# First up group by K tile, norms through a matrix of 1/2048, and later state outputs in a hybrid streaming step

## The chip, the core and the metric

The kernel runs on one core of one Trainium2 chip. The metric is the device time of one execution in microseconds. TensorE multiplies matrices into PSUM, VectorE (DVE), ScalarE (ACT) and GpSimd (POOL) work element by element, and the queues of SyncE (SP), GpSimd and ScalarE start transfers. Each engine takes its instructions in order and waits for the others through semaphores.

## What is computed

One layer of a streaming encoder for 256 prompt positions and 32 sample positions, held side by side as 288 columns (`NT`), with features on the partitions:

```python
xn = rmsnorm(x, norm_mix_pre)
proj = xn @ w_in                 # [pool 1024 | z 2048 | xBC 2560 | dt 32]
y_pool = pool_mixer(u, ...)      # trailing means, then four 256 x 256 products
y_ssd, new_conv, new_h = ssd_mixer(z, xbc, dt_raw, ...)   # grouped gated RMSNorm at its end
mix = concatenate([y_pool, y_ssd]) @ w_out
x = x + rmsnorm(mix, norm_mix_post)
hn = rmsnorm(x, norm_ffn_pre)
up = hn @ w_up                   # 2048 -> 2 * 5632
up, new_fconv = causal_dwconv(up, hist_fconv, ...)
f = (silu(gate) * val) @ w_down
x = x + rmsnorm(f, norm_ffn_post)
```

The outputs are `x` for both groups and the new caches, among them `new_h`, the SSD states of prompt and sample (128 x 2048 values each here).

## The kernel before

Products are made in fp32 precision from three passes: weights and activations are split into a rounded part (`hi`) and a remainder (`lo`), and `mm3` (L133) adds hi x hi, hi x lo and lo x hi. `fetch_w` (L110) loads a piece of weights into a `raw` tile on SP's queue, `split_w` (L116) makes `whi` on ScalarE and `wlo` on VectorE, 1024 columns at a time, each from a ring of four buffers. `project` (L138) runs a group of output tiles of 128 features over the K tiles in pieces `ksplit`, each tile into a bank of PSUM: five banks `acc` and three banks `aux`, which also hold the sums of norms and other small products.

The stages in order: the first six tiles of the input product, the SSD mixer beside the rest of that product, the pooling branch, the output product of the mixer (`wov`, eight groups of two tiles, L755), the residual and the norm before the FFN (L772 to L800), the FFN in two halves (`up_half`, L853, then the down product, L867 and L943), and the final norm.

Norms need the sum of squares over features, that is over partitions and tiles, for each of the 288 columns. `token_sums` (L472) multiplies the squares (as weights) with one column of `ones`, so that positions land on partitions; `token_rstd` (L483) takes root and reciprocal of three columns; `spread` (L490) turns the result back into 288 columns on all partitions; `copy_out` (L506) takes it out of PSUM where it is needed there. Two grouped norms of the SSD mixer (`rg`, L585 and L595), the norm behind the mixer (`p_m`, `rm`, L772) and the norm ahead of the FFN (`r2`, L800) go this way. The norm at the input (L233) multiplies the full matrix `ones` with the sums.

The states are 2048 columns in four parts j of 512. `state_in` (L709) fetches and scales the inputs through GpSimd's queue, `state_p` (L727) and `state_s` (L737) make the prompt's and the sample's part on TensorE and write them out on SP's queue. They run behind the mixer's output groups 2, 3 and 4; the last part is fetched behind group 6 and made between the sums and the spread of `rm`, with the order pinned (`keep_in_program_order`).

From there `s` runs over 16 feature tiles: x1 = mg * rm + x (two VectorE operations), `hn` in `hi` (ScalarE) and `lo` (VectorE), the square on ScalarE and its addition to `xsum` on VectorE. The first up group (L856) is six tiles in four pieces of four K tiles; it takes `hn` as it comes. Its results are multiplied by `r2` in `fconv` (L811), which is why the product may start ahead of the sums; then come the convolution, the gate (`finish_pair`, L829) and the split of `fa`. `blocks_out` (L167) transposes a finished x1 tile on VectorE into one buffer `blocks` and writes it to DRAM with four transfers, 16 times in the first half. Where several instructions can go, a scheduler sets each engine's order by priority: `ahead` brings weight splits forward, `EVAC` the operations that empty PSUM.

Of the kernel before, what the change touches and what calls it, by code (L numbers as in the profile page):

```python
# [16 lines left out]
P = 128  # L17
# [3 lines left out]
NS = 32  # L21
# [22 lines left out]
def body(  # L44
# [12 lines left out]
    w_out,  # L57
    w_up,
# [51 lines left out]
    def fetch_w(view, kb, nk, c0, nc_):  # L110
        raw = wpool.tile([P, nk, nc_], F32, tag="raw", name="raw")
        with tc.high_priority(offset=ahead[0]):
            sp.dma_start(out=raw, in_=view[:, c0 // 256, kb : kb + nk, :])
        return raw
# [52 lines left out]
    def blocks_out(d, t, src, pool_):  # L167
# [12 lines left out]
    ones = const.tile([P, P], F32, name="ones")  # L180
    pool.memset(ones, 1.0)
    tri = const.tile([P, P], F32, name="tri")
    pool.affine_select(
        out=tri, in_=ones, pattern=[[1, P]], compare_op=ALU.is_ge, fill=0.0, base=0, channel_multiplier=-1
# [47 lines left out]

    def input_rstd():  # L233
        p_ = aux([P, NT], "prs")
        pe.matmul(p_, ones, xsum, start=True, stop=True)
        act.activation(rstd, p_, AF.Sqrt, bias=eps_t, scale=1.0 / D_MODEL)
        dve.reciprocal(rstd, rstd)
# [187 lines left out]
    elast = const.tile([P, HEADS + 24], F32, name="elast")  # L425
# [46 lines left out]
    def token_sums(p_, sq, first_, last_, pin=False):  # L472


        for b, o in enumerate((0, P, NT - P)):
            ins = pe.matmul(
                p_[:, b : b + 1], sq[:, o : o + P], ones[:, 0:1],
                start=first_ and b == 0, stop=last_ and b == 2, skip_group_check=True,
            )
            if pin:  # L480
                tc.keep_in_program_order(ins)

    def token_rstd(p_, scale, name):  # L483

        o = const.tile([P, 3], F32, tag="trs", bufs=2, name=name)
        act.activation(o, p_[:, 0:3], AF.Sqrt, bias=eps_t, scale=scale)
        dve.reciprocal(o, o)
        return o

    def spread(rs, name, pin=False):  # L490

        p_ = aux([P, NT], name)
        for b, (o, n) in enumerate(BLK):
            ins = pe.matmul(
                p_[:, o : o + n], rs[:, b : b + 1].broadcast_to([P, P]), ident[:, P - n :], start=True, stop=True
            )
            if pin:
                tc.keep_in_program_order(ins)
        return p_

    def rstd_all(sq, scale, name):
        p_ = aux([P, 4], "psum_t")
        token_sums(p_, sq, True, True)
        return spread(token_rstd(p_, scale, name), name)

    def copy_out(p_, pool_, name):  # L506
        o = pool_.tile([P, NT], F32, tag="spread", bufs=3, name=name)
        act.activation(o, p_, AF.Copy)
        return o
# [63 lines left out]
    for i in range(NX // 2):  # L573
# [21 lines left out]
    rg.append(copy_out(rstd_all(gsum[1], 0.25 / 1024, "rg1"), const, "rg1_"))  # L595
# [141 lines left out]
    def state_s(j, x, h, pin=False):  # L737
# [7 lines left out]
    late_in = []  # L745

    def mix_before(g):
        def hook(kb, n):
            if g == 0 and kb == 0:
                pool_group(0)  # L750
            if g == 7 and kb == 0:
                token_sums(p_m, msum, True, False)
        return hook

    for grp in ((0, 1), (2,), (3,), (4,), (5,), (6,), (7,)):  # L755
# [4 lines left out]
        if 2 <= grp[0] < 5:  # L760
# [3 lines left out]
        elif grp[0] == 6:  # L764
            late_in = state_in(3)
# [11 lines left out]
    late = []  # L777
    for s in range(KD + 1):
        if s < KD:
            tc.keep_in_program_order(dve.tensor_tensor(x1[s], x1[s], rm, op=ALU.mult))  # L780
            tc.keep_in_program_order(dve.tensor_tensor(x1[s], x1[s], xT[:, s, :], op=ALU.add))
        if s:
            t = s - 1
            a = atile("hn")
            hi = act.activation(a[:, 0, :], x1[t], AF.Copy, scale=g_ffn_pre[:, t : t + 1])
            lo = dve.scalar_tensor_tensor(  # L786
                a[:, 1, :], x1[t], g_ffn_pre[:, t : t + 1], a[:, 0, :].bitcast(F32),
                op0=ALU.mult, op1=ALU.subtract,
            )
            tc.keep_in_program_order(lo)  # L790
            if t == 0:
                late.extend((hi, lo))
            if t == 0:
                act.activation(xsum, x1[t], AF.Square)
            else:
                q = op_.tile([P, NT], F32, tag="sq", bufs=2, name="sq")
                act.activation(q, x1[t], AF.Square)
# [254 lines left out]
```

## Time and profile before

| | us |
|---|---|
| median of 3 runs (1341.77 to 1343.39) | 1343.27 |
| the profiled execution | 1341.92 |
| its span, first to last instruction | 1340.2 |
| VectorE busy | 875.3 |
| ScalarE busy | 662.4 |
| GpSimd busy | 217.6 |

The profile comes from one execution on the hardware. A line of the chain of waits gives start, length, engine, what is written and the source line; a line of a timeline gives start, length, engine, line, operation, out<-in with partitions x elements, count, and in brackets how long the engine sat idle before and what ended it; a group of instructions gives busy time, mean ns of one and idle time. PE is TensorE, PEld its weight loads. An fp32 matmul without the split stands as two records.

### The profile page before, as it was taken

How to read it: one execution, taken by the hardware profiler on the slowest of the kernel's cores; microseconds unless marked ns; L12 is line 12 of the kernel's file. 1: busy time of each engine (PE TensorE's matmuls, PEld its weight loads, DVE VectorE, ACT ScalarE, POOL GpSimd, SP SyncE). 2: the span in 40 equal slices, each digit the busy share in tenths (PEclk: the TensorE clock that was granted, in tenths of full speed). 3: DMA queues.
4: the chain of work that ended last, by engine and by line, in shares of the span. 5: the costliest groups of instructions: out<-in, count | busy, mean ns of one | idle time of the engine just before them, and what ended most of it. 6: DMA issues, size and time to landing. Idle time of an engine off the chain costs nothing.

```text
span 1340.2 us, 25164 instructions
## 1 busy us (share of the span) xinstructions
PE 1316.9 (98%) x10089; PEld 1299.9 (97%) x10089; DVE 875.3 (65%) x1453; ACT 662.4 (49%) x995; POOL 217.6 (16%) x348
## 2 busy tenths in 40 slices
PE   7999999999999999999999999999999999999996
PEld 7999999999999998999999999999999999999995
DVE  7898997688544477876676643435666666664443
ACT  7558776446443456545445433334444444454441
POOL 6221111120221101211121100001111111101110
PEclk9999999999999999999999999999999999999998
DMA  7668875365656346765544444554544544566652
GB/s 285 229 197 267 286 232 167 133 232 200 229 200 216 111 126 187 230 180 178 178 158 168 171 149 168 171 181 164 183 157 163 185 158 162 177 229 198 197 165 89
DMA packets 104585, 249.82 MB, mean 186 GB/s; under 512 B 63812, under 2 KB 69508, under 8 KB 81812
## 3 DMA queue, kind: packets, MB, share of 16 engines
q1 hardware_dynamic: 102416, 242.85, 55.3%
q0 software_dynamic: 1488, 4.92, 1.0%
q8 instruction: 79, 1.29, 0.4%
q10 hardware_dynamic: 564, 0.45, 0.1%
q14 instruction: 38, 0.31, 0.1%
HBM read 236.23 MB, written 11.95 MB: 185 GB/s over the span
## 4 chain that ended last, share of the span: by engine, by line
PE 95%; DVE 3%; issue 1%; DMA 1%; ACT 0%; SPq 0%; DVEq 0%
PE acc L136 31%; PE acc L134 30%; PE acc L135 30%; PE py L461 1%; DMA raw<-in_w_first 1%; PE pst L730 1%; DVE wlo L129 0%; DVE xn L98 0%; DVE wlo L265 0%; DVE xr L968 0%; DVE hn L786 0%; PE psts L739 0%; PE py L463 0%; PE acc_x L136 0%; DVE xsum L798 0%
## 5 line engine op out<-in xcount | busy, mean ns | idle before, releaser
L129 DVE TENSOR_TENSOR wlo<-raw,whi 128x1024 fp32r<-128x1024 f32 (+1 forms) x400 | 479.7, 1201 | 345.3 <-ACT whi L128 344.4
L128 ACT ACTIVATE whi<-raw 128x1024 fp32r<-128x1024 f32 (+1 forms) x400 | 414.3, 1037 | 491.4 <-PE acc L135 397.6
L136 PE MATMUL acc<-hn,wlo 128*128 128x288 f32 x1392 | 413.0, 298 | 0.9 <-DVE wlo L129 0.9
L134 PE MATMUL acc<-hn,whi 128*128 128x288 f32 x1392 | 403.7, 293 | 2.3 <-ACT whi L128 2.2
L135 PE MATMUL acc<-hn,whi 128*128 128x288 f32 x1392 | 403.3, 291 | 0.0
L134 PEld LDWEIGHTS acc<-hn,whi 128*128 128x128 f32 x1392 | 259.9, 188 | 4.0 <-ACT whi L128 3.3
L136 PEld LDWEIGHTS acc<-hn,wlo 128*128 128x128 f32 x1392 | 261.2, 188 | 2.1 <-DVE wlo L129 1.6
L135 PEld LDWEIGHTS acc<-hn,whi 128*128 128x128 f32 x1392 | 261.3, 188 | 0.7 <-DVE hn L786 0.5
L134 PE MATMUL acc<-xn,whi 128*128 128x288 f32 x688 | 203.4, 297 | 6.3 <-ACT whi L264 6.3
L136 PE MATMUL acc<-fa,wlo 128*128 128x288 f32 x704 | 209.3, 297 | 0.0
L134 PE MATMUL acc<-fa,whi 128*128 128x288 f32 x704 | 206.1, 293 | 0.0
L135 PE MATMUL acc<-fa,whi 128*128 128x288 f32 x704 | 204.2, 290 | 0.0
L135 PE MATMUL acc<-xn,whi 128*128 128x288 f32 x688 | 200.7, 293 | 0.0
L136 PE MATMUL acc<-xn,wlo 128*128 128x288 f32 x688 | 198.6, 297 | 0.7 <-DVE wlo L265 0.7
L134 PEld LDWEIGHTS acc<-xn,whi 128*128 128x128 f32 x688 | 130.1, 189 | 7.4 <-ACT whi L264 6.6
L134 PEld LDWEIGHTS acc<-fa,whi 128*128 128x128 f32 x704 | 132.2, 188 | 0.0
L136 PEld LDWEIGHTS acc<-fa,wlo 128*128 128x128 f32 x704 | 132.2, 188 | 0.0
L135 PEld LDWEIGHTS acc<-fa,whi 128*128 128x128 f32 x704 | 132.1, 188 | 0.0
L135 PEld LDWEIGHTS acc<-xn,whi 128*128 128x128 f32 x688 | 130.0, 189 | 0.1
L136 PEld LDWEIGHTS acc<-xn,wlo 128*128 128x128 f32 x688 | 127.8, 189 | 1.5 <-DVE wlo L265 0.9
L818 POOL COPY fc_stage<-ebuf 128x4 f32<-128x4 f32 x88 | 27.8, 316 | 531.4 <-DVE ebuf L817 531.4
L814 POOL COPY ebuf<-pf 128x2 f32<-128x2 f32 x88 | 71.6, 814 | 134.6 <-DVE fc L824 69.2
(264 smaller groups left out, 1585.5 us busy)
## 6 DMA issues: line engine op xcount, KB each, us to landing
raw<-in_w_up SPq DMA_DIRECT2D x82, 1024.0 KB, 4.8
raw<-in_w_in SPq DMA_DIRECT2D x38, 1024.0 KB, 5.1
raw<-in_w_down SPq DMA_DIRECT2D x32, 1024.0 KB, 4.8
raw<-in_w_out SPq DMA_DIRECT2D x24, 1024.0 KB, 4.8
raw<-in_w_down SPq DMA_DIRECT2D x16, 768.0 KB, 4.2
gb<-g_d SPq DMA_DIRECT2D x8, 832.0 KB, 6.8
raw<-in_w_up SPq DMA_DIRECT2D x12, 512.0 KB, 3.5
raw<-in_w_first SPq DMA_DIRECT2D x7, 768.0 KB, 9.8
```

Source lines behind the costliest of these rows:

```text
L128: act.activation(hi, raw[:, k : k + n, :], AF.Copy)
L129: dve.tensor_tensor(lo, raw[:, k : k + n, :], hi.bitcast(F32), op=ALU.subtract)
L134: pe.matmul(out, wh, a[:, 0, :], start=start, stop=False)
L135: pe.matmul(out, wh, a[:, 1, :], start=False, stop=False)
L136: pe.matmul(out, wl, a[:, 0, :], start=False, stop=stop)
L461: pe.matmul(y[:, 0:256], xw[:, 0, c], m[:, j, 0:256], start=True, stop=False)
L730: ins = pe.matmul(st, btok[:, j // 2, b, :], x[:, b, :], start=b == 0, stop=b == 1)
L814: pool.tensor_copy(e[:, 258:260], pf[:, 4:6, i])
L818: pool.tensor_copy(fc_stage[:, :, :, i], e[:, 256:324].rearrange("p (s c) -> p s c", c=34)[:, :, 0:2])
```

## The change

The first up group has seven tiles and goes K tile by K tile, from a weight array `w_up1` that the host has put together (896 columns), with the eighth tile in `w_up2`; the rest of `w_up` is shifted accordingly. Its residual for tile k+1 is made ahead of the split of tile k, and the squares are added on GpSimd. Four norms (`rg` twice, `rm`, `r2`) multiply the full matrix `mean` of 1/2048 with the squares and take root and reciprocal of all 288 columns. The state parts j = 2 and 3 are both made behind the mixer's last sums, and a sample's state is copied out by ScalarE and added on GpSimd.

```diff
-    ones = const.tile([P, P], F32, name="ones")
-    pool.memset(ones, 1.0)
+    mean = const.tile([P, P], F32, name="mean")
+    pool.memset(mean, 1.0 / D_MODEL)
...
+    def root(o, p_, scale=1.0):
+        act.activation(o, p_, AF.Sqrt, bias=eps_t[: p_.shape[0]], scale=scale)
+        return dve.reciprocal(o, o)
...
-    elast = const.tile([P, HEADS + 24], F32, name="elast")
+    elast = const.tile([P, HEADS + 32], F32, name="elast")
...
+    def gate_rstd(t):
+        p_ = aux([P, NT], "psum_g")
+        pe.matmul(p_, mean, gsum[t], start=True, stop=True)
+        o = const.tile([P, NT], F32, tag="spread", bufs=3, name="rg")
+        root(o, p_, 0.5)
         return o
...
-            rg.append(copy_out(rstd_all(gsum[0], 0.25 / 1024, "rg0"), const, "rg0_"))
+            rg.append(gate_rstd(0))
...
-    p_m = aux([P, 4], "psum_m")
-    tc.keep_in_program_order(act.activation(warm, eps_t, AF.Sqrt))
+    p_m = aux([P, NT], "psum_m")
...
-        if m == KD - 1:
-            for i, q in enumerate(last_sq):
-                token_sums(p_m, q, False, i == 1, pin=True)
+        if m == KD - 2:
+            pe.matmul(p_m, mean, q, start=False, stop=False)
...
-        dve.tensor_tensor(h, h, st, op=ALU.add)
-        sp.dma_start(out=new_ssd_s[:, 512 * j : 512 * j + 512], in_=h)
+        ho = stp[0].tile([P, 512], F32, tag="ho", bufs=2, name="hos")
+        act.activation(ho, st, AF.Copy)
+        pool.tensor_tensor(ho, ho, h, op=ALU.add)
+        sp.dma_start(out=new_ssd_s[:, 512 * j : 512 * j + 512], in_=ho)
...
-                token_sums(p_m, msum, True, False)
+                pe.matmul(p_m, mean, msum, start=True, stop=False)
...
-        if 2 <= grp[0] < 5:
+        if 2 <= grp[0] < 4:
...
-        elif grp[0] == 6:
-            late_in = state_in(3)
+        elif 4 <= grp[0] < 6:
+            late_in[grp[0] - 2] = state_in(grp[0] - 2)
...
-    rm_t = token_rstd(p_m, 1.0 / D_MODEL, "rm")
-    state_s(3, *late_in, pin=True)
-    rm = spread(rm_t, "rm", pin=True)
-    state_p(3, *late_in, pin=True)
+    state_s(3, *late_in[3], pin=True)
+    tc.keep_in_program_order(pe.matmul(p_m, mean, last_sq[1], start=False, stop=True))
+    state_p(3, *late_in[3], pin=True)
+    state_s(2, *late_in[2], pin=True)
+    state_p(2, *late_in[2], pin=True)
+    rm = const.tile([P, NT], F32, tag="spread", bufs=3, name="rm")
+    tc.keep_in_program_order(root(rm, p_m))
     hn = []
...
+    up1 = [(aux([P, NT], "acc_x") if m in (3, 4) else acc_ps.tile([P, NT], F32, tag="acc", name="acc")) for m in range(7)]
...
+    residual(0)
+    for k in range(KD):
+        if k % 2 == 0:
+            raw = wpool.tile([P, 2, 896], F32, tag="raw", name="raw")
+            with tc.high_priority(offset=ahead[0]):
+                sp.dma_start(out=raw, in_=w_up1[:, k : k + 2, :])
+        if k + 1 < KD:
+            residual(k + 1)
+        a = atile("hn")
+        hi = act.activation(a[:, 0, :], x1[k], AF.Copy, scale=g_ffn_pre[:, k : k + 1])
+        lo = dve.scalar_tensor_tensor(
+            a[:, 1, :], x1[k], g_ffn_pre[:, k : k + 1], a[:, 0, :].bitcast(F32), op0=ALU.mult, op1=ALU.subtract
+        )
...
-                dve.tensor_tensor(xsum, xsum, q, op=ALU.add)
+            pool.tensor_tensor(xsum, xsum, q, op=ALU.add)
...
+        whi, wlo = wtile("hi", 1, 896)[:, 0, :], wtile("lo", 1, 896)[:, 0, :]
+        with ExitStack() as order:
+            order.enter_context(tc.high_priority(offset=ahead[0]))
+            if k > 1:
+                order.enter_context(tc.issue_after(hi.ins))
+                order.enter_context(tc.issue_after(lo.ins))
+            act.activation(whi, raw[:, k % 2, :], AF.Copy)
+            dve.tensor_tensor(wlo, raw[:, k % 2, :], whi.bitcast(F32), op=ALU.subtract)
+        for m in range(7):
+            c = slice(m * P, (m + 1) * P)
+            mm3(up1[m], whi[:, c], wlo[:, c], a, k == 0, k == KD - 1)
+    p_ = aux([P, NT], "psum_t")
+    pe.matmul(p_, mean, xsum, start=True, stop=True)
+    r2 = const.tile([P, NT], F32, tag="spread", bufs=3, name="r2")
+    root(r2, p_)
...
             if j == 0:
-                up((0, 0, 2), (0, 1, 0), 1)
+                for m, (kind, t) in enumerate(((0, 0), (0, 1), (1, 0), (1, 1))):
+                    conv_[kind, t] = fconv(kind * NF + t, up1[m])
+            elif j == 2:
+                for m, (kind, t) in enumerate(((0, 2), (0, 3), (1, 2))):
+                    conv_[kind, t] = fconv(kind * NF + t, up1[4 + m])
+                up(1, 3, w_up2)
...
+    rf = const.tile([P, 3], F32, name="rf")
+    root(rf, p_f[:, 0:3])
```

`residual(t)` holds the same two operations on x1 as before, multiplication by `rm` and addition of x, both pinned in their order.

More of the change, by code (lines that the diff above doesn't have):

```diff
@@ L231, in input_squares @@
             pool.tensor_tensor(xsum, xsum, q, op=ALU.add)
+    def root(o, p_, scale=1.0):
+        act.activation(o, p_, AF.Sqrt, bias=eps_t[: p_.shape[0]], scale=scale)
+        return dve.reciprocal(o, o)
     def input_rstd():
         p_ = aux([P, NT], "prs")
-        pe.matmul(p_, ones, xsum, start=True, stop=True)
-        act.activation(rstd, p_, AF.Sqrt, bias=eps_t, scale=1.0 / D_MODEL)
-        dve.reciprocal(rstd, rstd)
+        pe.matmul(p_, mean, xsum, start=True, stop=True)
+        root(rstd, p_)
     act.dma_start(out=g_mix_pre, in_=g0_in)
@@ L470, in ssd_four @@
             dve.scalar_tensor_tensor(xs[t], xs[t], dcol[:, t : t + 1], ys[i], op0=ALU.mult, op1=ALU.add)
[L472 to L508, printed above, removed]
+    def gate_rstd(t):
[3 more added lines that the diff above has]
+        root(o, p_, 0.5)
         return o
@@ L769, in body @@
             act.dma_start(out=new_pool, in_=np_stage)
-    rm_t = token_rstd(p_m, 1.0 / D_MODEL, "rm")
-    state_s(3, *late_in, pin=True)
-    rm = spread(rm_t, "rm", pin=True)
-    state_p(3, *late_in, pin=True)
-    hn = []
[L777 to L797, printed above, removed]
-                dve.tensor_tensor(xsum, xsum, q, op=ALU.add)
-            hn.append(a)
@@ L801, in body @@
+    p_ = aux([P, NT], "psum_t")
+    pe.matmul(p_, mean, xsum, start=True, stop=True)
+    r2 = const.tile([P, NT], F32, tag="spread", bufs=3, name="r2")
+    root(r2, p_)
     x1d = dram.tile([NT, D_MODEL], F32, name="x1d")
@@ L838, in body, with up @@
     conv_ = {}
-    def up(js, kinds, spare=0):
-        cols = [(kind * D_FF + j * P, 256) for j, kind in zip(js, kinds)]
+    def up(kind, j, view=None):
         def out(m, p_):
-            j, kind = js[m // 2] + m % 2, kinds[m // 2]
-            conv_[kind, j] = fconv(kind * NF + j, p_)
-        project(
-            wuv, cols, hn, K16 if js[0] else [(0, 4), (4, 4), (8, 4), (12, 4)], done=out, spare=spare,
-            hold=() if js[0] else tuple(late),
-        )
+            conv_[kind, j + m] = fconv(kind * NF + j + m, p_)
+        project(*((view, [(0, P)]) if view is not None else (wuv, [(kind * (D_FF - 512) + j * P - 512, 256)])), hn, K16, done=out)
     def up_half(lo_, hi_):
```

43 lines of the change are left out of this document (29 added, 14 removed).

## The prediction

> **What bounds the kernel now.** Three views, in this order: the page, the chain of waits, then TensorE's instructions by window and by time.
>
> ```profile
> span 1340.2 us, 25164 instructions
> PE 1316.9 (98%) x10089; PEld 1299.9 (97%) x10089; DVE 875.3 (65%) x1453; ACT 662.4 (49%) x995; POOL 217.6 (16%) x348
> ...
> PE 95%; DVE 3%; issue 1%; DMA 1%; ACT 0%; SPq 0%; DVEq 0%
> ```
> TensorE is busy for 98% of the span and 95% of the chain lies on it, so only two things change the time: TensorE's own instructions, and the places where it waits. The profiled execution took 1341.92 us for this span; the median of the runs shown is 1343.27, 1.35 us more.
>
> The steady price of one 288-column matmul is read between two events: the first matmul on `fa` and the next one on `hn`, with 16 tiles x 22 K tiles x 3 = 1056 matmuls between them.
>
> ```profile
> 769.62 0.29 PE L134 MATMUL acc<-fa,whi 128*128 128x288 f32 x1
> ...
> 908.07 0.29 PE L134 MATMUL acc<-hn,whi 128*128 128x288 f32 x1
> ```
> (908.07 - 769.62) / 1056 = 0.1311 us. "Busy" hides short waits, as each record lasts 0.29 us; the pitch doesn't. After the mixer's last matmul, at 479.59, the trace has this:
>
> ```profile
> 484.00:500.00 16.00, 15.91 (x111) 1.00 0.40 120
> 500.00:515.00 15.00, 12.68 (x82) 1.00 0.35 99
> 515.00:530.00 15.00, 13.09 (x95) 1.00 0.70 218
> ```
> ```profile
> 479.59 1.33 PE psum_m L476 x12
> 480.92 0.97 PE psts L739 x2
> 481.88 0.59 PE rm L494 x6
> 482.47 1.80 PE pst L730 x4
> ...
> 516.80 0.58 PE psum_t L476 x6
> ...
> 521.75 0.59 PE r L494 x6
> ```
> The window rows (start and end, length, TensorE's busy time and its instruction count, clock, DMA) count the first up group's matmuls. At 0.1311 us a window of 15 us holds 114; the middle one has 82. From 479.59 to 769.62 stand 44 tiles x 48 = 2112 matmuls, 276.9 us of the 290.0. The other 13.1 us are the chain's rows: 4.7 us of sums, states and spread (1.33 + 0.97 + 0.59 + 1.80), 1.2 us for `r2` (0.58 + 0.59), and so 7.3 us of waiting. This stretch is what the change rebuilds; outside it, TensorE's only waits of note are in the first tiles, which don't change.
>
> Why it waits: in one K tile VectorE does two residual operations, `lo`, the sum `xsum` and three quarters of a 1024-wide `wlo`. Their pitches in the chain:
>
> ```profile
> 495.56 1.14 DVE wlo L129
> 496.70 0.37 DVE mg L781
> 497.06 0.43 DVE hn L786
> ```
> 3 x 0.37 + 0.43 + 0.75 x 1.14 = 2.40 us, against 18 x 0.1311 = 2.36 us on TensorE, and in coarse steps of four K tiles. VectorE feeds too slowly.
>
> **The change part by part.** TensorE's fp32 work first.
>
> ```profile
> 40.98 0.48 PE prs L235 x2
> ...
> 218.42 0.76 PE psum_t L476 x6
> ...
> 225.48 0.59 PE rg L494 x6
> ...
> 274.60 0.56 PE psum_t L476 x6
> ...
> 280.12 0.59 PE rg L494 x6
> ...
> 419.69 1.72 PE pst L730 x4
> 421.41 0.86 PE psts L739 x2
> ```
> A 288-wide fp32 matmul is two records, 0.48 us (`prs`). Both gate norms lose token sums and spread: 0.76 + 0.59 + 0.56 + 0.59 = 2.50 us become 2 x 0.48, so -1.54 us, in places where TensorE never waits. Their full-width reciprocals load VectorE by about 2 us each (price below); the ring of four weight tiles, split ahead of TensorE, covers that, and without the cover it would cost at most those 2 us each. Moving the states of j = 2 takes 1.72 + 0.86 = 2.58 us out of the mixer's output; they come back below. The inputs of j = 2 and 3 are now fetched right behind the groups 4 and 5; their three transfers each stand in GpSimd's queue ahead of `msum` adds, as those of j = 0 to 2 did before, and on SP's queue nothing moves but the output writes.
>
> The front, from T = the end of the mixer's last matmul. On TensorE in the changed order: states of the sample j = 3 (0.86), two sums by `mean` (0.96), prompt j = 3 (1.72), sample j = 2 (0.86), prompt j = 2 (1.72): 6.12 us of cover. Against it run two chains.
>
> ```profile
> L785 ACT ACTIVATE hn<-mg,par 128x288 fp32r<-128x288 f32 x16 | 8.5, 532 | 10.5 <-DVE mg L781 10.4
> L237 DVE RECIPROCAL rstd<-rstd 128x288 f32<-128x288 f32 x1 | 2.0, 1956 | 0.6 <-ACT rstd L236 0.6
> L734 ACT ACTIVATE ho<-pst 128x512 f32<-128x512 f32 x4 | 2.4, 591 | 0.3
> ```
>
> ```profile
> 43.25 0.50 ACT L236 ACTIVATE rstd<-prs,eps_t 128x288 f32<-128x288 f32 x1
> ```
> (1) Sums end at T+1.82; Sqrt over 288 columns 0.50; reciprocal 1.96, where the old one was three columns; T+4.3. VectorE's order then has three multiplications before the first addition, 3 x 0.37 + 0.45; T+5.85. `hn` on ScalarE 0.53; T+6.4. (2) ScalarE's queue holds the copy `hos` of j = 2 ahead of that `hn`, and it waits for a write: the four state copies share two buffers, `ho`, and the third takes the first one's, which GpSimd must add to and the queue must write out.
>
> ```profile
> 440.23 0.81 POOL L518 TENSOR_TENSOR msum<-msum,sq 128x288 f32<-128x288 f32 x1 [17.66 <-ACT sq L517]
> 442.55 1.49 POOL L518 TENSOR_TENSOR msum<-msum,sq 128x288 f32<-128x288 f32 x1 [1.51 <-ACT sq L517]
> ```
>
> ```profile
> DMA to landing us min/median/max: 2.4/6.0/6.7
> ```
> First copy ends T+1.5. The GpSimd add over 512 columns isn't in the trace: 0.81 x 512/288 = 1.44 us from the shorter row, 1.49 x 512/288 = 2.65 from the longer; I take 1.44, as VectorE then runs a one-input reciprocal. T+3.0. The write lands after 2.4 to 6.7 us; I take 2.4, since the weight buffers are filled by then and nothing is queued. T+5.4; copy 0.59, `hn` 0.53: T+6.6. So the second chain ends last, by little, and the wait is 0.5 us. Behind the waiting copy stand `hn`, the squares and `whi`, hence everything. The seventh tile's bank needs the last `ho` copy: 0.2 more. Front: 6.8 us.
>
> The group itself: 21 x 0.1311 = 2.75 us on TensorE per K tile. VectorE: 2 x 0.37 + 0.43 + 1.14 x 896/1024 = 2.17, plus what GpSimd's `xsum` adds do to it. The start of the kernel has both at once:
>
> ```profile
> 19.73 4.02 POOL L231 TENSOR_TENSOR xsum<-xsum,xsq 128x288 f32<-128x288 f32 x4
> ```
>
> ```profile
> 18.79 4.30 DVE L98 SCALAR_TENSOR_TENSOR xn<-xT,g,xn 128x288 fp32r<-128x288 f32 x6
> ```
> Six `lo` operations took 4.30 us instead of 6 x 0.43 = 2.58, beside four adds: 0.43 us an add. The bounds are 0 (no interference) and 1.0 (the whole add, 4.02 / 4). I take 0.43, the row with the same operations: 2.60, under 2.75. TensorE then sets the pace. VectorE's lead at the third tile is some 1.8 us: by ScalarE's queue its `wlo` is done at T+11.2, and TensorE reaches it at 6.8 + 2 x 2.75 + 0.7 = T+13. I put 0.4 us for the beginning. [...]
>
> The end, from U = the group's last matmul. Seven tiles hold all five `acc` banks and two `aux`; the eighth takes `psum_t`. The next tile, `up(1, 3)`, needs `up1[0]`'s bank, so `r2` must be finished and used first; TensorE's order has nothing else. In the old order the same chain ran behind remaining matmuls of the group, and its rows give the prices:
>
> ```profile
> 516.71 1.06 ACT L128 ACTIVATE whi<-raw 128x1024 fp32r<-128x1024 f32 x1 [3.08 <-PE acc L135]
> ```
>
> ```profile
> 517.46 0.48 DVE L170 STREAM_TRANSPOSE blocks<-mg 128x288 f32<-128x288 f32 x1 [2.01 <-PE psum_t L476]
> 517.86 1.18 DVE L129 TENSOR_TENSOR wlo<-raw,whi 128x1024 fp32r<-128x1024 f32 x1
> ...
> 522.82 0.42 DVE L816 TENSOR_TENSOR ebuf<-acc,r__5960 128x256 f32<-128x256 f32 x1 [3.69 <-ACT r__5960 L508]
> 523.16 0.18 DVE L817 TENSOR_TENSOR ebuf<-acc,r__5960 128x32 f32<-128x32 f32 x1
> ```
>
> ```profile
> 518.01 1.32 SPq L173 DMA_DIRECT2D x1d<-blocks  x3
> ```
>
> ```profile
> DMA to landing us min/median/max: 1.5/3.1/5.5
> ```
> In the changed order the last `whi` before the Sqrt waits for the weights of K tile 15: ScalarE U+0.2 to 1.3, Sqrt to 1.8. VectorE's order is `blocks`, the `wlo` of that `whi` (1.3 to 2.4), reciprocal (to 4.4), a second `blocks`, and only then `up1[0]`. That second `blocks` shares one buffer with the first and waits for its four writes: first one done U+1.1, four issues of 0.44, last at 2.45, landing 1.5 to 5.5 later, median 3.1; with nothing large ahead in the queue but one weight load I take 2.45: U+4.9. Transpose 0.4 and the two evacuating operations, 0.34 + 0.18, to 5.8; TensorE resumes at U+6.0, its 0.48 of `psum_t` included. Bounds: 5.4, where the reciprocal ends last, and 9.0, with a landing of 5.5.
>
> Sum of the stretch: 6.8 + 0.4 + 6.0 = 13.2 against 13.1. The waits keep their size and change place. What is gained is fp32 work: -2.58 - 1.54 = -4.12. I add 0.5 for VectorE's crowded queue after U, where six more evacuations and seven convolutions stand before the next `wlo` (bounds 0 and 1.5). Together -3.5 us: 1338.4 for the profiled execution, 1339.8 beside the median.
>
> **The rivals.** All times beside the median.
> A. GpSimd's adds make VectorE the bound. If each add holds VectorE for 1.0 us, its length in the start, a K tile needs 3.17, 0.42 over TensorE; 14 x 0.42 - 1.8 of lead = 4.0 us, and at U three `wlo` still stand before the reciprocal, 1.5 more. Less the 0.4 counted: +5.1, 1344.9, slower. At 0.81, the shorter add of the mixer, it is 2.98 a tile: 14 x 0.23 - 1.8 = 1.4, and 0.4 at U, 1341.6. For it: 4.30 us in place of 2.58, and 1.49 beside 0.81. Against: the six operations took 0.43 an add. It decides from 0.58 an add and ends slower than before from about 0.9. Chance 0.10 for each of the two sizes. [...]
> B. The write of the first `hos` lands after the median 6.0 us: the front grows by 3.6, 1343.4, no change. For: the median. Against: the empty queue. Every microsecond over 2.4 counts. Chance 0.16.
> C. The ends go well: the `blocks` writes land in 1.5 (-0.6), no crowding (-0.5), no loss at the beginning (-0.4): 1338.3. Chance 0.15.
> D. The group doesn't do what its shape says: waits are those of latency between engines, not of VectorE's sum, and some 3 us of them stay inside: 1342.4. For: ScalarE has its `sq`, `hn` and `whi` in one queue too. Against: 2.17 leaves room. Chance 0.07.
>
> **How the numbers follow.** The forecast has 0.42, with its own range 1338.0 to 1341.5. A run's spread makes 0.2%, 2.7 us, the least that can be told from no change. Faster: three quarters of the forecast and C, some of D: 0.49. Same: the rest of the forecast, most of B and D, and the smaller A: 0.32. Slower: the larger A, and B or a late `blocks` write on top of adds that cost 0.6: 0.19. The range 1337.0 to 1345.0 takes in C and both sizes of A, and leaves out two mishaps at once.
>
> **What would show it.** Right: between the mixer's last matmul and `fa` the matmuls on `hn` come at 2.75 us per K tile; one wait of TensorE under 1 us before `hn`, one of about 5.5 us before the first matmul of the tile after the seven, with VectorE waiting there for `whi`, then for `x1d`'s writes; gate sums of 0.48 us. Wrong: ScalarE's `hos` waiting over 3 us for `out` (B); `hn` matmuls waiting for `wlo` in each K tile, and VectorE's `mg` and `wlo` longer than before (A). Most of all the forecast falls if the wait after the seven tiles is under 3 us or over 9.

## The result, and the profile after

The changed kernel takes 1350.27 us (median of four executions, 1349.61 to 1351.51) beside 1343.08 for the kernel before (1341.77 to 1343.39): a ratio of 1.0056, 95% interval 1.0039 to 1.0074. The forecast was 1339.8. The profiled execution took 1349.65 us, so it is 11.3 us over the 1338.4 that the sum gave for it. One execution behind the medians of this document, in experiment 7, took 2180.24 us at a mean granted clock of 0.557 and is left out there.

The page of the changed kernel, and its TensorE timeline: all rows from the pooling stage to `fa` in which TensorE sat idle for more than 0.25 us, and the first `fa` matmul.

```profile
span 1347.6 us, 25068 instructions
...
PE 1316.1 (98%) x10041; PEld 1300.7 (97%) x10041; DVE 884.1 (66%) x1436; ACT 664.9 (49%) x997; POOL 234.8 (17%) x368
```
```profile
290.03 0.53 PE L136 MATMUL acc<-du,whi 128*128 128x288 f32 x2 [3.39 <-ACT du L95]
...
486.71 0.66 PE L136 MATMUL acc<-hn,whi 128*128 128x288 f32 x3 [0.45 <-ACT hn L770]
...
489.12 0.40 PE L137 MATMUL acc<-hn,whi 128*128 128x288 f32 x1 [1.20 <-DVE hn L771]
...
541.71 0.58 PE L136 MATMUL acc<-hn,whi 128*128 128x288 f32 x1 [7.06 <-DVE ebuf L813]
...
777.28 0.29 PE L136 MATMUL acc<-fa,whi 128*128 128x288 f32 x1
```
TensorE is "busy" for 1316.1 us, 0.8 less than before, and yet the span is 7.4 us longer. The four waits are 12.1 us together; the two short ones stand in one place, so there are three stalls. The chain of waits gives the prices of what TensorE does, and the times T (the mixer's last matmul ends, 480.13) and U (the group's last one, 534.16):

```profile
218.30 0.68 PE psum_g L480 x2
...
273.56 0.48 PE psum_g L480 x2
...
480.13 0.86 PE psts L711 x2
...
534.16 0.50 PE psum_t L794 x2
...
542.29 0.24 PE acc L137
```
The last row shows something that the waits don't: a matmul at a pitch of 0.24 us instead of 0.1311. The windows of TensorE (start and end, length, busy time and count, granted clock, DMA share, GB/s), cut where the clock changes, say when:

```profile
288.04:291.46 3.42, 1.43 (x11) 1.00 0.62 249
291.46:294.87 3.41, 3.41 (x17) 0.50 0.00 0
...
486.02:489.43 3.41, 1.76 (x10) 1.00 0.40 150
489.43:492.84 3.41, 3.41 (x16) 0.50 0.01 4
...
533.80:537.22 3.42, 0.85 (x5) 1.00 1.00 419
537.22:540.63 3.41, 0.00 (x0) 0.50 1.07 284
...
544.04:547.46 3.42, 3.42 (x16) 0.50 0.07 11
547.46:550.87 3.41, 3.41 (x28) 1.00 0.22 37
```
Behind each of the three stalls the granted clock is 0.50, for one, one and three windows of 3.41 us. In such a window TensorE is fully "busy" and does half the work: 16 or 17 records where 28 stand at full clock. The loss is 1 - 0.1311 / 0.24 = 0.45 us for each microsecond of work at half clock: 1.55 us for a full window, and 0.45 x (547.46 - 541.71) = 2.6 us at the third place. 5.7 us in all, and the kernel before has no such window between these stages.

Two stretches show where the 7.4 us lie. The mixer's last matmul ends at 480.13, 0.54 later than before (479.59), though some 4 us of fp32 work were taken out ahead of it. From there to `fa` it is 777.28 - 480.13 = 297.15 us, against 290.0: 7.1 more. Behind `fa` it is 0.2 less.

**The first stall**: VectorE in the pooling stage, after (first fence) and before (second).

```profile
276.54 1.95 DVE L238 RECIPROCAL rg<-rg 128x288 f32<-128x288 f32 x1
...
279.33 2.31 DVE L640 TENSOR_TENSOR xs<-xs,rg 128x288 f32<-128x288 f32 x6
...
281.97 0.81 DVE L640 TENSOR_TENSOR xs<-xs,rg 128x288 f32<-128x288 f32 x2
...
289.04 0.41 DVE L616 SCALAR_TENSOR_TENSOR dpool<-win,ubuf 128x256 f32<-128x256 f32 x1
```
```profile
281.19 1.56 DVE L666 TENSOR_TENSOR xs<-xs,rg__3579 128x288 f32<-128x288 f32 x4
282.67 0.41 DVE L642 SCALAR_TENSOR_TENSOR dpool<-win,ubuf 128x256 f32<-128x256 f32 x1
```
Before, the first `dpool` was ready at 283.1, and TensorE had matmuls on `xn` until the pooling product began at 288.4. After, VectorE does the reciprocal of 1.95 us and, since `rg` now comes without spread and copy, all eight multiplications of `xs` ahead of the pooling windows; `dpool` is ready at 289.4, and TensorE has been idle since 286.6.

**The second**: the front of the up group, three engines.

```profile
485.79 1.43 POOL L716 TENSOR_TENSOR hos<-hos,sh 128x512 f32<-128x512 f32 x1 [2.82 <-ACT hos L715]
```
```profile
485.11 0.60 ACT L715 ACTIVATE hos<-psts 128x512 f32<-128x512 f32 x1 [0.80 <-DMA out<-hos]
```
```profile
486.00 1.53 DVE L758 TENSOR_TENSOR mg<-mg,rm 128x288 f32<-128x288 f32 x1
487.46 1.18 DVE L759 TENSOR_TENSOR mg<-mg,xT 128x288 f32<-128x288 f32 x3
488.56 0.51 DVE L771 SCALAR_TENSOR_TENSOR hn<-mg,par,hn 128x288 fp32r<-128x288 f32 x1
```
The chain over `hos` came as forecast: the copy waits only 0.80 for the write, and `hn` begins at T+6.58. But `lo(0)` stands behind a fourth multiplication and three more additions, and that multiplication, 0.37 us of pitch by itself, takes 1.45 while GpSimd's addition of 512 columns runs.

**The third**: VectorE at the group's end, and the row of the chain of waits that holds it.

```profile
536.30 1.94 DVE L238 RECIPROCAL r<-r 128x288 f32<-128x288 f32 x1
540.68 0.48 DVE L172 STREAM_TRANSPOSE blocks<-mg 128x288 f32<-128x288 f32 x1 [2.44 <-DMA x1d<-blocks]
```
```profile
536.56 4.00 DMA x1d<-blocks
```
The order on VectorE is the forecast one. The last of the four writes lands 4.00 us after its issue, not 2.45, while 419 and 284 GB/s move in the two windows there; TensorE resumes at U+7.55.

Inside the group the 0.4 us of the forecast hold, but with nothing to spare:

```profile
520.73 1.06 DVE L758 TENSOR_TENSOR mg<-mg,rm 128x288 f32<-128x288 f32 x1
```
```profile
519.87 1.60 POOL L780 TENSOR_TENSOR xsum<-xsum,sq 128x288 f32<-128x288 f32 x1 [0.38 <-ACT sq L779]
```
In each K tile a VectorE operation of 0.45 us lasts about 1.06 beside GpSimd's addition: 0.6 us an add, between the 0.43 taken and the 0.81 and 1.0 of rival A, and VectorE then needs 2.8 us against TensorE's 2.75. The same multiplication, without an addition beside it, has 0.45 at 517.88.

### The profile page after: what moved, and what is told of

Read it like the earlier page. It is cut to its first block, busy times and chain, and to the rows that moved or that the text cites. A ratio compares the mean times of both kernels' runs of the same rounds, so it can differ in the third digit from the quotient of the medians.

```text
span 1347.6 us, 25068 instructions
## 1 busy us (share of the span) xinstructions
PE 1316.1 (98%) x10041; PEld 1300.7 (97%) x10041; DVE 884.1 (66%) x1436; ACT 664.9 (49%) x997; POOL 234.8 (17%) x368
## 3 DMA queue, kind: packets, MB, share of 16 engines
q1 hardware_dynamic: 101840, 242.85, 54.9%
q8 instruction: 78, 1.28, 0.4%
## 4 chain that ended last, share of the span: by engine, by line
PE 95%; DVE 2%; DMA 1%; ACT 0%; issue 0%; SPq 0%; DVEq 0%; ACTq 0%
PE acc L138 31%; PE acc L136 30%; PE acc L137 30%; PE py L467 1%; DVE xn L100 1%; DMA raw<-in_w_first 1%; PE acc_x L138 0%; DVE wlo L271 0%; PE acc_x L137 0%; PE acc_x L136 0%; DVE xr L963 0%; DMA x1d<-blocks 0%; PE py L469 0%; PE pst L702 0%; DVE mg L758 0%
## 5 line engine op out<-in xcount | busy, mean ns | idle before, releaser
L131 DVE TENSOR_TENSOR wlo<-raw,whi 128x1024 fp32r<-128x1024 f32 (+1 forms) x386 | 463.4, 1201 | 335.6 <-ACT whi L130 334.7
L130 ACT ACTIVATE whi<-raw 128x1024 fp32r<-128x1024 f32 (+1 forms) x386 | 399.6, 1036 | 475.6 <-PE acc L137 383.2
```

What stands on the lines that cost most here:

```text
L130: act.activation(hi, raw[:, k : k + n, :], AF.Copy)
L131: dve.tensor_tensor(lo, raw[:, k : k + n, :], hi.bitcast(F32), op=ALU.subtract)
```

## The experiments

Eleven kernels, each compared with the kernel before, whose medians beside them were 1342.4 to 1342.9. A single execution of a kernel lies up to 3.5 us from its median, once 4.9, so places are read from the traces, and totals from medians. "Less than the changed kernel" compares with the 1350.27 above, which was not timed again beside them; its ratio is known to 0.0017 either way, so a difference of under some 2.4 us to it is not shown by the totals alone.

**1. The multiplications by `rg` behind the pooling tiles.**

```diff
-        for t in range(8 + 2 * n, 10 + 2 * n):
-            dve.tensor_tensor(xs[t], xs[t], rg[1], op=ALU.mult)
...
-            pool_tile(2 * i + 3)
+            du = pool_tile(2 * i + 3)
+            if n == 1:
+                with tc.issue_after(du.ins):
+                    for t in range(8, NX):
+                        dve.tensor_tensor(xs[t], xs[t], rg[1], op=ALU.mult)
```
`pool_tile` now returns the instruction that makes `lo` of `du`, and the multiplications are put behind it.

> The changed kernel with the eight multiplications of xs by the second gate norm (rg) moved on VectorE behind the first pair of pooling tiles; nothing else. Theory: the pooling stage lost its time because these eight, 0.4 us each, came ahead of the pooling windows as soon as rg was ready early; TensorE's wait of 3.39 us for du at 286.6 and the half clock behind it (about 1.55 us) then vanish together: 4.9 us less than the changed kernel, about 1345.4. Rival 1: the full-width reciprocal of 1.95 us is what delays du; then the wait shrinks by 1.2 us at most, to 1349. Rival 2: the wait goes, but the clock falls to half there anyway: 3.4 us less, 1346.9.

Measured: 1344.5 us, ratio to the kernel before 1.0014 (1.0005 to 1.0023). Timelines of TensorE and VectorE:

```profile
287.43 0.43 PE L136 MATMUL acc<-du,whi 128*128 128x288 f32 x2
```
```profile
277.50 1.94 DVE L238 RECIPROCAL rg<-rg 128x288 f32<-128x288 f32 x1
...
290.74 3.03 DVE L645 TENSOR_TENSOR xs<-xs,rg 128x288 f32<-128x288 f32 x8
```
No idle time stands before `du`, the clock stays at 1.00, and the reciprocal is still there: rivals 1 and 2 fall. Moving the eight multiplications is enough to remove the wait, with the reciprocal left where it was. The total is 5.8 us less than the changed kernel's, where 4.9 was expected. From the first gate sum to the mixer's end the stretch is now 4.2 us shorter than before, which is what the forecast promised for the whole part (4.12).

**2. The gate norms back to column sums and spread**, with all else changed.

```diff
-            rg.append(gate_rstd(0))
+            rg.append(copy_out(rstd_all(gsum[0], 0.5, "rg0"), const, "rg0_"))
...
-    rg.append(gate_rstd(1))
+    rg.append(copy_out(rstd_all(gsum[1], 0.5, "rg1"), const, "rg1_"))
```
`token_sums`, `token_rstd`, `spread` and `copy_out` are those of before, on one column of `mean`.

> The changed kernel with the two gate norms alone back to column sums, three-column reciprocals and the spread; first up group, states and the other norms stay changed. Theory (VectorE's order behind the early rg): the wait for du and its half clock go (-4.9 us), the fp32 work comes back (+1.3 us): 3.6 us less than the changed kernel, about 1346.7. Rival (the gate norms were a gain, as forecast, and the time in the pooling stage went elsewhere): 1.3 us more, about 1351.6.

Measured: 1345.89 us (1.0020, 1.0011 to 1.0030), 0.8 less than expected, and no idle time before `du`. It undoes the part in another way and says the same. The difference to the first experiment, 1.4 us in both the medians and the stretch, is the fp32 work of the two norms.

**3. The gate norms by `mean` alone**, in the kernel before.

```diff
-            rg.append(copy_out(rstd_all(gsum[0], 0.25 / 1024, "rg0"), const, "rg0_"))
+            rg.append(gate_rstd(0))
```


> The kernel before with one part of the change alone: the two gate norms by the matrix mean, with full-width root and reciprocal. As forecast blind, -1.3 to -1.5 us against before, about 1341.7. Theory (VectorE's order behind the early rg): the wait of some 3.4 us for du appears here as well, with a half clock of about 1.5 us behind it: +3.6 us, about 1346.7.

Measured: 1348.13 us (1.0043, 1.0029 to 1.0057), 5.3 more than the kernel before beside it. TensorE's timeline and windows:

```profile
292.80 0.53 PE L134 MATMUL acc<-du,whi 128*128 128x288 f32 x2 [3.39 <-ACT du L93]
```
```profile
515.18:518.59 3.41, 2.06 (x12) 1.00 0.01 5
518.59:522.00 3.41, 3.41 (x15) 0.50 0.76 245
```
One edit that takes 1.4 us of work away makes the kernel slower, by the same wait of 3.39 us. In this execution there is a second window at half clock, in the old first up group: its short waits, which the clock of the kernel before survived, here add up to 1.35 us in one window. That would be the rest over my 3.6, but the profiled execution took 1353.01 us and is not typical; whether the others have this window no trace shows.

**4. The lo products of K tile 0 last.**

```diff
-        for m in range(7):
+        for w_, b_ in ((whi, 0), (wlo, 0), (whi, 1)) if k == 0 else ():
+            for m in range(7):
+                ins = pe.matmul(up1[m], w_[:, m * P : (m + 1) * P], a[:, b_, :], start=w_ is whi and b_ == 0, stop=False)
+                tc.keep_in_program_order(ins)
+        for m in range(7 if k else 0):
...
```


> The changed kernel, in which K tile 0 of the first up group runs its seven hi x hi first, then seven with wlo, and the seven that need lo(0) last, so that TensorE has 14 matmuls to do while lo(0) is late; the same 21 matmuls. Theory: the half clock from 489.4 to 492.9 follows TensorE's wait of 1.20 us for lo(0); without that wait the clock stays at 1.00: -1.2 -1.6 = 2.8 us less than the changed kernel, about 1347.5. Rival: the clock falls because of the sparse stretch of state products and the wait of 0.45 for hn ahead of it, whatever K tile 0 does: 1.2 us less at most, about 1349.1, with the granted clock at 0.50 for some 3.4 us as before.

Measured: 1349.32 us (1.0042, 1.0027 to 1.0056), 0.95 less than the changed kernel, which is within the noise. TensorE's timeline, and the chain of waits at the group's end:

```profile
491.18 0.66 PE L792 MATMUL acc<-hn,whi 128*128 128x288 f32 x3 [0.27 <-DVE hn L771]
...
543.96 0.58 PE L136 MATMUL acc<-hn,whi 128*128 128x288 f32 x1 [9.34 <-DVE ebuf L817]
```
```profile
536.54 6.26 DMA x1d<-blocks
```
The wait is down from 1.20 to 0.27, and no window at half clock follows. From the first `hn` matmul to `psum_t` it is 45.2 us instead of 47.3: 2.1 are gained. At the group's end 2.3 are given back, 9.34 instead of 7.06: the write now takes 6.26 us to land. The total lies nearer to the rival's but doesn't separate the two; the trace is the theory's, and the gain went into another wait. Experiment 1, whose front stays at full clock, shows the same: its end wait is 8.49, and its chain there has

```profile
531.22 5.31 DMA x1d<-blocks
```
From the first `hn` matmul to the resumption behind the group it is 55.2 us here, 54.9 in experiment 1 and 55.0 in the changed kernel. So in these traces, where the end waits for that write, TensorE resumes no sooner without the wait for `lo(0)`, or without the half clock behind it.

That the clock stays up here is no proof that this wait had brought it down: experiment 1 has 0.45 and 1.20 us unchanged and keeps its clock too. The last section takes it up.

**5. `r2` ahead of K tile 15's matmuls.**

```diff
+        if k == KD - 1:
+            p_ = aux([P, NT], "psum_t")
+            pe.matmul(p_, mean, xsum, start=True, stop=True)
+            r2 = const.tile([P, NT], F32, tag="spread", bufs=3, name="r2")
+            root(r2, p_)
         for m in range(7):
...
-    p_ = aux([P, NT], "psum_t")
...
-    root(r2, p_)
```


> The changed kernel with the sum, root and reciprocal of r2 placed ahead of K tile 15's matmuls; the squares are complete by then. VectorE then runs blocks, a wlo, the reciprocal, a wlo and goes on to the first tile's results, with no second transpose in between. Theory: TensorE's wait of 7.06 us behind the seven tiles was the reciprocal's chain and, at its end, a second transpose that waits for the first one's writes; with both out of the way TensorE resumes about 3.5 us after the group's last matmul instead of 7.5: 4 us less, and up to 2.7 us more if the clock then stays at 1.00: 1343.6 to 1346.3. Rival: the wait is one for the next weights (wlo) or for the evacuation itself; then it stays near 7 us and the time near 1350.

Measured: 1343.82 us (1.0003, 0.9994 to 1.0013), 6.5 less than the changed kernel. TensorE's timeline and windows:

```profile
537.06 0.38 PE L136 MATMUL acc<-hn,whi 128*128 128x288 f32 x1 [2.80 <-DVE ebuf L814]
```
```profile
486.38:489.80 3.42, 2.23 (x10) 1.00 0.36 136
489.80:493.21 3.41, 2.95 (x22) 1.00 0.24 90
```
The wait is 2.80 instead of 7.06, with one window at half clock behind it instead of three. The total is at the low end of the expected 1343.6 to 1346.3, but not by the end alone: the wait is 4.26 us shorter and the half clock behind it costs 1.1 less, and another 1.55 comes from the front, which in this execution stays at full clock without any edit there. The window rows show why: the wait of 1.20 for `lo(0)` is there, but lies across two windows, so the front is not slowed.

**6. A second transpose buffer.**

```diff
-                blocks_out(x1d, t, x1[t], fp)
+                blocks_out(x1d, t, x1[t], fp, blocks_b if t % 2 else None)
```


> The changed kernel with a second transpose buffer in the first FFN half, so that the second transpose needs no landed write. Theory: it waits 2.4 to 4.7 us for the four writes of the first (the landing takes about 4 to 6 us from the first issue, not the 2.45 us taken in the forecast); without it the first result is out when the reciprocal ends, about 5 us after the group's last matmul: 2.4 us less, about 1347.9, with the clock at 0.50 behind it as before. Rival: the first write's landing isn't what holds it; no change, 1350.3.

`blocks_out` takes the buffer as an argument now; `blocks_b` is the second one.

Measured: 1346.26 us (1.0022, 1.0011 to 1.0033), 4.0 less than the changed kernel. In TensorE's timeline the wait is

```profile
537.67 0.58 PE L136 MATMUL acc<-hn,whi 128*128 128x288 f32 x1 [4.30 <-DVE ebuf L815]
```
so 2.8 us shorter: U+4.8 instead of 7.55, under the 5.4 that the forecast had for the reciprocal ending last. The write's landing held the second transpose, and that the results. The rest of the 4.0 is not in this trace's group end (2.6 us are still lost at half clock there); this execution had no half-clock window in the front.

**7. TensorE kept at work through the wait.**

```diff
+    fill = aux([P, NT], "fill")
+    for i in range(36):
+        pe.matmul(fill, whi[:, 0:P], a[:, 0, :], start=i == 0, stop=i == 35)
     x1d = dram.tile([NT, D_MODEL], F32, name="x1d")
```


> The changed kernel with 36 matmuls added behind psum_t that nothing reads (into the eighth bank, from the last K tile's operands), so that TensorE works for some 4.7 us of the wait of 7 us. Nothing else is changed, so the wait ends at the same time. Theory: the clock goes to 0.50 behind this wait because TensorE is idle, and the half clock costs about 2.7 us after the resumption; with the fill it stays at 1.00: 1347.6. Rival 1: the half clock has another cause than idleness; it stays at 0.50 for 10.24 us, 1350.3. Rival 2: the fill delays the tile behind it: longer than 1350.3.

Measured: 1344.46 us (1.0015, 1.0005 to 1.0025). Windows and timeline of TensorE:

```profile
535.19:538.60 3.41, 2.82 (x20) 1.00 1.02 423
538.60:542.01 3.41, 3.41 (x28) 1.00 0.45 106
```
```profile
536.54 5.07 PE L799 MATMUL fill<-hn,whi 128*128 128x288 f32 x36 [0.59 <-ACT r L237]
541.44 0.30 PE L136 MATMUL acc<-hn,whi 128*128 128x288 f32 x1
...
774.32 0.29 PE L136 MATMUL acc<-fa,whi 128*128 128x288 f32 x1
```
With 36 matmuls that nobody reads the kernel is 5.8 us faster than the changed one. The clock stays at 1.00, and from the resumption at 541.44 to `fa` it is 232.9 us, where the changed kernel needs 777.28 - 541.71 = 235.6: the half clock cost 2.7 us there, and idleness is its cause. "Nothing else is changed" was wrong, though: the scheduler put the reciprocal on VectorE ahead of a `wlo` and the first results ahead of the second transpose, so they were out before the fill ended, and TensorE resumed 1.6 us sooner after U as well. The total is not evidence for the clock alone; the 232.9 is.

**8. The states' additions on VectorE.**

```diff
-        ho = stp[0].tile([P, 512], F32, tag="ho", bufs=2, name="hos")
-        act.activation(ho, st, AF.Copy)
-        pool.tensor_tensor(ho, ho, h, op=ALU.add)
-        sp.dma_start(out=new_ssd_s[:, 512 * j : 512 * j + 512], in_=ho)
+        dve.tensor_tensor(h, h, st, op=ALU.add)
+        sp.dma_start(out=new_ssd_s[:, 512 * j : 512 * j + 512], in_=h)
```


> The changed kernel in which the sample's states are added on VectorE straight out of PSUM, as in the kernel before (no ScalarE copy hos, no GpSimd add of 512 columns, two fewer users of the two ho buffers). Theory: the second GpSimd add stretches one residual multiplication from 0.45 to 1.53 us and so makes lo(0) late; without it TensorE's wait of 1.20 us for lo(0) all but goes, and hn starts no later: 1 to 1.5 us less, and 1.5 us more where that wait brought the half clock: 1347.3 to 1349.3. Rival: VectorE's two extra additions of 512 columns from PSUM, some 0.6 us each, land in the same chain and eat the gain: 1350.3 or more.

Measured: 1352.08 us (1.0063, 1.0046 to 1.0079), 1.8 more than the changed kernel, which is within the noise, and not the 1 to 3 less that was expected: a miss. VectorE and TensorE:

```profile
485.69 0.69 DVE L714 TENSOR_TENSOR sh<-sh,psts 128x512 f32<-128x512 f32 x1 [2.86 <-PE psts L711]
486.30 1.95 DVE L238 RECIPROCAL rm<-rm 128x288 f32<-128x288 f32 x1
```
```profile
490.47 1.02 PE L136 MATMUL acc<-hn,whi 128*128 128x288 f32 x3 [3.10 <-ACT hn L768]
```
The stretched multiplication is gone, as expected: 0.45 us at 489.76, not 1.53. But the addition for j = 2 stands in VectorE's queue ahead of `rm`'s reciprocal and waits 2.86 us for its product, so `hn` comes 2.6 us later. It is the waiting, not the 0.69 us, that costs; the change's way over GpSimd is no worse than this one.

**9. The additions to `xsum` on VectorE.**

```diff
-            pool.tensor_tensor(xsum, xsum, q, op=ALU.add)
+            dve.tensor_tensor(xsum, xsum, q, op=ALU.add)
```


> The changed kernel with the additions to xsum on VectorE instead of GpSimd. Theory: beside each GpSimd add one VectorE operation of 0.45 us takes about 1.06, so an add on GpSimd costs VectorE some 0.6 us; on VectorE it costs 0.37 to 0.45 itself. VectorE's sum per K tile goes from about 2.8 to about 2.6 us, against 2.75 on TensorE: the time between the group's first and last matmul is the same within 0.3 us, and the total within 1 us of 1350.3. Rival (GpSimd's adds make VectorE the bound, the prediction's rival A): the group becomes shorter by 1.4 us or more.

Measured: 1347.33 us (1.0034, 1.0022 to 1.0046), 2.9 less. In the trace the group's first `hn` matmul and `psum_t` are 47.5 us apart, in the changed kernel 47.3: the interior didn't become shorter, so rival A falls, although no VectorE operation there is stretched any more (multiplications, additions and `xsum` at 0.45 to 0.46 us from 497.24 on). The gain came from elsewhere, and I hadn't expected it:

```profile
539.47 0.58 PE L136 MATMUL acc<-hn,whi 128*128 128x288 f32 x1 [4.30 <-DVE ebuf L813]
```
In this order the first results stand ahead of the second transpose, and the end wait is that of experiment 6.

**10 and 11. The edits together**: the first, the fourth and the fifth, and then with 12 matmuls of fill behind the group.

```diff
+    for i in range(12):
+        pe.matmul(fill, whi[:, 0:P], a[:, 0, :], start=i == 0, stop=i == 11)
```


> The changed kernel with three of the edits together: the multiplications by the second gate norm behind the first pooling tiles, r2 ahead of K tile 15's matmuls, and K tile 0 of the first up group with its lo products last. Theory (three waits of TensorE, each with a clock penalty, are all that the change lost): from the changed kernel -4.9 for the first, -6.5 for the second as it measured alone, about -1.0 for the third: 1337.9, and faster than the kernel before by about 5 us. In the trace: no wait for du, under 1 us of waits ahead of the second K tile, about 2.8 us behind the seven tiles with one or two windows at 0.50 behind it. Rival: gains ahead of the group's end are given back there, as the edit of K tile 0 alone showed (its end wait was 2.3 us longer, as the first transpose's writes landed later): 1340 or more.

> The three edits together, and 12 matmuls that nothing reads behind the group's last one, which keep TensorE busy for 1.6 us of the wait there; they also move the first results on VectorE right behind the reciprocal, ahead of one wlo of 1.17 us. Theory: TensorE resumes about 1.8 us after the group's last matmul instead of 3, and is idle for only 0.3 us, so the clock stays at 1.00 (-1.6): 2.8 us less than with three edits, about 1335.1. Rival: the wlo that was put back is what TensorE waits for next; the same time as with three edits.

Measured: 1338.71 us with three edits (0.9969, 0.9957 to 0.9981) and 1336.0 with the fill (0.9950, 0.9937 to 0.9962), beside 1342.4 for the kernel before. A window of TensorE with all four:

```profile
530.12:533.53 3.41, 2.70 (x21) 1.00 0.99 356
```
TensorE resumes in this window, 2.5 us after the group's last matmul, and of these it is idle for 0.71; the clock stays at 1.00, and no window at half clock is left between the first stage and the last 15 us. Both medians are within 1 us of what the theory gave. So what the change lost lies in the first stall and at the group's end; without them it does more than the 3.5 us promised, 6.4, in part because the end now takes less than the 6.0 us that the forecast had counted (2.5). The gain expected of K tile 0's edit, 1.0, is not shown: experiment 5 less the 4.9 of the first stall is 1338.9 already. About 4.2 of these lie ahead of the mixer's end, as in experiment 1, and 2.2 between it and `fa`.

## Why the prediction was wrong

**The fp32 work (-1.54 and -2.58): right.** The sums were 0.68 and 0.48 us, and experiment 1 has both gains, 4.2 us together; the second experiment has the first alone, 1.4.

**"The ring of four weight tiles, split ahead of TensorE, covers that, and without the cover it would cost at most those 2 us each": this step failed.** It looked at the added load on VectorE and at one customer, the weights. It didn't ask what an earlier `rg` sets free. Eight multiplications that had been spread between the pooling windows all became ready first and went ahead of them, and this held up `du`, for which TensorE waits. Price: 3.39 + 1.55 = 4.9 us, shown by experiments 1 to 3 (taken away twice, put into the old kernel once). "In places where TensorE never waits" was true of the old order only.

**The front, 6.8 us: the forecast chain was right (6.58), the one beside it was missing.** GpSimd's addition was priced by when it ends, and not by what it does to VectorE while it runs; nor were the fourth multiplication and the later additions counted ahead of `lo(0)`. Price in this execution: 1.20, and 1.55 of half clock. Experiment 4 took the wait down to 0.27 and gained nothing by it in the end, because the group's end waits for a write (55.2 us against 55.0); so this price is one of bookkeeping, and what the front costs by itself is open. That GpSimd's addition of 512 columns would take the shorter of two lengths, "as VectorE then runs a one-input reciprocal", was the author's estimate: the first one took 1.27 us, at 481.70, with VectorE idle until the reciprocal began at 482.53, so what a reciprocal does to an addition is not shown.

**The group, 0.4 us of loss: right,** with 0.6 us an add instead of 0.43. The stretched operations end 0.3 us behind the additions, at 521.79 and 487.53 against 521.47 and 487.22. They began 0.86 and 0.21 us into them, so an add cost 0.6 and 1.1 us, not its full 1.60 and 1.43. Rival A, which took the full length, didn't come: experiment 9. (Its smaller size, worked like the larger, less the 0.4 counted, would have been 1341.2, not 1341.6.)

**The end, U+6.0: one term was mis-sized.** "With nothing large ahead in the queue but one weight load I take 2.45" for the landing; it was 4.00, and 5.31 and 6.26 where the group took less time: within the bounds of 1.5 to 5.5 in the changed kernel, over them in experiment 4. The trace of the kernel before had the nearest row: the 5.5 is the landing of this very write, the last of the first tile's four, issued at 519.87. Price: 1.55 in this execution; experiments 5 and 6 show that the wait hangs on it. Behind it 2.6 us of half clock, shown by experiment 7.

**The clock was in no term.** Half clock behind the three stalls makes 5.7 of the 11.3 us. The range's upper end, 1345.0, was made of waits alone, and is passed by these. The windows of the kernel before all read 1.00 where it waited 0.4 to 0.7 us at a time (1.09 us in one window at most, 508.49 to 511.90), and the forecast took its new waits of 0.5 and 5.5 us as if nothing followed.

The other rivals: B didn't come (the copy waited 0.80, not over 3), nor C; of D's waits for latency inside the group the trace has none. The wait behind the seven tiles, 7.06, lay inside the 3 to 9 that was to decide; what fell was named nowhere.

Sum: 4.9 + 2.75 + 1.55 + 2.6 = 11.8, less the 0.5 for a crowded queue, which didn't come (from the resumption to `fa` it is 235.6 - 2.6 = 233.0 us, and 37 tiles x 48 x 0.1311 = 232.8): 11.3, as measured. It says where the time of this execution lies. Of the two middle terms only the sum holds: each grows as the other shrinks.

## What to carry to other kernels

Something that becomes ready earlier is a change of order on every engine that uses it: list what it frees and what that goes ahead of. Price a wait of TensorE with the clock behind it, here 0.45 us for every microsecond of work until the clock was back, and give TensorE any matmul it can do meanwhile, useful or not: 36 that nobody read kept the clock at 1.00 in experiment 7. A result that the next stage waits for must not stand behind an instruction that waits for a landed write, and a gain just ahead of such a place is given back there, as in experiment 4: 2.1 us gained, 2.3 given back.

## What the runs showed of the hardware

The clock fell and rose at the borders of windows of 3.41 us that didn't move with the work: in the changed kernel's trace the three stretches at 0.50 that the work met begin at 291.46, 489.43 and 537.22, which are 58 and 14 times 3.413 us apart, and last 3.41, 3.41 and 10.24 us. TensorE's idle time in windows of this length at full clock, each given by its run and start:

| what followed | TensorE idle in the window, us |
|---|---|
| clock 0.50 | changed kernel: 1.99 (288.04), 1.65 (486.02), 2.57 (533.80); experiment 3: 2.90 (289.90), 1.35 (515.18); experiment 5: 2.80 (534.17); experiment 7: 1.66 (487.40); experiment 9: 1.66 (486.40) |
| clock 1.00 | kernel before: 1.09 (508.49); changed kernel: 1.40 (284.63); experiment 2: 1.28 (481.86); experiment 5: 1.19 (486.38); experiment 8: 1.46 (534.94) |

So in these windows it was the sum that decided, up to an unsharp border between 1.28 and 1.65 us, and where the windows began. The kernel's last windows don't fit: there the clock fell behind 0.49 us of idle time in the kernel before (1324.28 to 1327.69) and 0.84 in the changed one (1332.52 to 1335.94), and these windows hold matmuls of 1 and 128 columns as well; why, no run shows. The same pair of waits, 0.45 and 1.20 us, makes 1.65 in the changed kernel's window at 486.02 and brings the clock down; in experiment 5 the border at 489.80 splits it into 1.19 and 0.46, and the clock stays. In each of the changed kernel's three stretches at half clock it was back at 1.00 behind the first window that TensorE worked through (up to 294.87, 492.84 and 547.46).

The landing of the same four small writes took 4.00, 5.31 and 6.26 us from the last issue in the changed kernel and experiments 1 and 4, longer where the group had been shorter: 47.3, 45.8 and 45.2 us from the first `hn` matmul to `psum_t`. That weight loads in flight are the reason is a guess: it fits the DMA share of 1.00 and the 419 GB/s in the changed kernel's window there, but no run took them away.
